# A row-wise maximum that ignores NaN: the first tile loaded as 16 and then 112 partitions

## The chip, the cores and the metric

The kernel runs on one core of a Trainium2 chip. The metric is device time in microseconds, from runs of the whole program; the median of three runs is given. The profile is of one execution, whose own time stands beside its span.

## The reference

```python
x = np.random.randn(32, 2048, 2048).astype(np.float32)
x[np.random.rand(32, 2048, 2048) < 0.1] = np.nan
np.nanmax(x, axis=-1).astype(np.float32)
```

65,536 rows of 2,048 floats (537 MB) are reduced to one float each: the largest value of the row that is not NaN. A tenth of the values is NaN.

## The kernel before

The whole input passes once through the core's on-chip memory (SBUF, 128 partitions). Each partition owns 512 rows, taken in two groups that lie one behind the other in memory (`source`, line 267). A *unit* is 256 floats, 1 KB in a partition; a row has 8 units. A *tile* is a stretch of units in all 128 partitions, at most 64 units: 64 KB in each partition, 8 MB in all. `TILES` (lines 16 to 25) lists the tiles in order. A tile is a list of loads, and a load is a tuple of steps: `(24, 40)` is one load of 64 units that is cleaned in two steps. There are 52 tiles of one load and one step at the start, the first of 16 units, the second of 48, then fifty of 64. After them the tiles have more and smaller loads, so that little work is left after the last one.

Three buffers `xt0` to `xt2` of 64 KB a partition take the tiles in turn (`number % BUFS`, line 372). For each load there are three stages:

- **Load.** SyncE (SP) issues the DMA (`load`, lines 252 to 265; the profile's line 258). A load waits until the last maximum over the tile that held the buffer before it is done (`free`, line 447), and 14 semaphores are used in turn for landings. The loads of the first `AHEAD = 3` tiles wait for nothing and are issued ahead of all else, before a barrier of the five engines (lines 273 to 286).
- **Clean.** `clean` (called in lines 396 and 397) rewrites the upper 16 bits of each float so that a NaN becomes something smaller than every number, while the order of the others is kept. ScalarE (ACT, line 295) does the first half of a step's columns, GpSimd (POOL, line 306) the second half, side by side. Both wait for the landing of the step's load.
- **Maximum.** VectorE (DVE, line 302) takes the maximum over each row's cleaned floats, one instruction for all whole rows of a step (line 431): `128x8 f32<-128x16384 f32` is eight rows in each partition. It waits for POOL's and ACT's cleaning, which count on one semaphore per step ("pair").

At the tiles that `SETTLE` (line 34) names, POOL turns finished maxima back into floats and marks rows of NaN alone; the keys are tile numbers, the values the number of tiles whose maxima are settled there. At the end a small matrix product sums the marks, two stores go out on SP, and a branch would take a slow general path if there were an infinite value or a row of NaN alone.

The order of instructions on each engine is that of the loop over tiles in line 363; the class `Order` puts in the semaphore waits, and nothing is rescheduled. The line that the change begins with is

```python
    [[(16,)], [(48,)]]
    + [[(64,)]] * 50
```

## Time and profile before

| | |
|---|---|
| runs | 1246.35 us median of 3 (1246.26 to 1246.93) |
| profiled execution | 1246.26 us, span 1244.4 us |
| VectorE, ScalarE, GpSimd busy | 1105.9, 603.7, 606.6 us |
| read from memory | 536.87 MB, 432 GB/s over the span |
| loads of 8 MB | 53 of the 102 DMAs, 31.3 us from issue to landing (median) |

A row of the timeline reads: start, length, engine, line of the kernel, operation, what it writes and reads, shapes, and in brackets the idle time of the engine just before it with what ended that time. "SPq" is the issuing of DMAs by SP. The chain of waits gives start, length and what the time went to. The landing of a load has no row of its own; it is seen where ACT's cleaning of it begins.

### The profile page before, as it was taken

How to read it: one execution, taken by the hardware profiler on the slowest of the kernel's cores; microseconds unless marked ns; L12 is line 12 of the kernel's file. 1: busy time of each engine (PE TensorE's matmuls, PEld its weight loads, DVE VectorE, ACT ScalarE, POOL GpSimd, SP SyncE). 2: the span in 40 equal slices, each digit the busy share in tenths (PEclk: the TensorE clock that was granted, in tenths of full speed). 3: DMA queues.
4: the chain of work that ended last, by engine and by line, in shares of the span. 5: the costliest groups of instructions: out<-in, count | busy, mean ns of one | idle time of the engine just before them, and what ended most of it. 6: DMA issues, size and time to landing. Idle time of an engine off the chain costs nothing.

```text
span 1244.4 us, 572 instructions
## 1 busy us (share of the span) xinstructions
PE 0.2 (0%) x2; PEld 0.1 (0%) x2; DVE 1105.9 (89%) x136; ACT 603.7 (49%) x131; POOL 606.6 (49%) x138
## 2 busy tenths in 40 slices
PE   0000000000000000000000000000000000000000
PEld 0000000000000000000000000000000000000000
DVE  1789889898898988988989889898898999999999
ACT  3354453553534535445354453544535536545556
POOL 3354453543534535445354453544535536545556
DMA  9999999999999999999999999999999999999999
GB/s 404 438 438 438 438 438 438 419 423 438 438 438 438 438 438 430 415 436 438 438 438 438 438 438 421 421 438 438 438 438 438 438 432 419 443 424 430 429 425 375
DMA packets 14688, 537.14 MB, mean 432 GB/s; under 512 B 1760, under 2 KB 1888, under 8 KB 4704
## 3 DMA queue, kind: packets, MB, share of 16 engines
q1 hardware_dynamic: 14688, 537.14, 99.9%
HBM read 536.87 MB, written 0.26 MB: 432 GB/s over the span
## 4 chain that ended last, share of the span: by engine, by line
DMA 50%; DVE 34%; POOL 14%; SPq 2%; issue 0%; ACT 0%; PE 0%
DMA xt<-in_x_dram 50%; DVE acc L302 33%; POOL xt L306 14%; SPq L258 2%; DVE parts L302 1%; POOL late L306 0%; ACT sums L295 0%; PE sums L460 0%; SPq L95 0%
## 5 line engine op out<-in xcount | busy, mean ns | idle before, releaser
L302 DVE TENSOR_REDUCE acc<-xt 128x8 f32<-128x16384 f32 (+5 forms) x95 | 1059.4, 11186 | 134.0 <-POOL xt L306 133.7
L306 POOL TENSOR_SCALAR xt<-xt 128x8192 uint16<-128x8192 int16 (+11 forms) x125 | 602.7, 4836 | 635.0 <-DMA xt<-in_x_dram 635.0
L295 ACT ACTIVATE xt<-xt 128x8192 uint16<-128x8192 int16 (+11 forms) x125 | 601.5, 4839 | 635.2 <-DMA xt<-in_x_dram 635.2
L302 DVE TENSOR_REDUCE parts<-xt 128x1 f32<-128x2048 f32 (+6 forms) x32 | 42.6, 1410 | 0.0
L302 DVE TENSOR_REDUCE xt<-xt 128x1 f32<-128x768 f32 (+1 forms) x4 | 3.7, 944 | 0.0
L302 DVE MEMSET small<- 128x1 f32 x2 | 0.1, 59 | 3.0 <-PEq L286 3.0
L295 ACT ACT_TABLE_LOAD x1 | 1.3, 1283 | 2.9 <-PEq L286 2.9
L306 POOL TENSOR_SCALAR low<-acc 128x312 f32<-128x312 f32 (+2 forms) x3 | 1.9, 626 | 0.2
L306 POOL TENSOR_SCALAR acc<-acc 128x312 uint16<-128x312 uint16 (+3 forms) x4 | 1.4, 343 | 0.3
L295 ACT ACTIVATE sums<-sums 1x22 f32<-1x22 f32 x1 | 0.1, 140 | 1.1 <-PE sums L460 1.1
L295 ACT ACTIVATE low<-low 128x491 f32<-128x491 f32 x1 | 0.6, 585 | 0.0
L460 PE MATMUL sums<-late,small 128*1 128x22 f32 x2 | 0.2, 200 | 1242.4 <-POOL late L306 1242.4
L306 POOL TENSOR_SCALAR late<-acc 128x19 f32<-128x19 f32 x1 | 0.3, 266 | 0.1
L306 POOL TENSOR_SCALAR late<-xt 128x2 f32<-128x2 f32 x1 | 0.2, 218 | 0.1
L460 PEld LDWEIGHTS sums<-late,small 128*1 128x1 f32 x2 | 0.1, 80 | 1242.4 <-issue 1242.4
L523 POOL MEMSET const-float32-0.0<- 128x1 f32 x1 | 0.1, 99 | 0.2 <-issue 0.2
L295 ACT ACTIVATE small<-small 128x1 f32<-128x1 f32 x1 | 0.2, 203 | 0.0
L302 DVE TENSOR_SCALAR acc<-acc 128x2 uint16<-128x2 uint16 x1 | 0.2, 171 | 0.0
L302 DVE TENSOR_REDUCE acc<-parts 128x19 f32<-128x57 f32 x1 | 0.2, 200 | 0.0
L295 ACT ACTIVATION_READ_ACCUMULATOR low<-low 128x1 f32 x1 | 0.2, 187 | 0.0
L295 ACT ACTIVATION_READ_ACCUMULATOR sums<-sums 1x1 f32 x1 | 0.2, 185 | 0.0
L302 DVE MEMSET parts<- 128x63 f32 x1 | 0.1, 111 | 0.0
(3 smaller groups left out, 0.3 us busy)
## 6 DMA issues: line engine op xcount, KB each, us to landing
xt<-in_x_dram SPq DMA_DIRECT2D x2, 7168.0 KB, 30.9
xt<-in_x_dram SPq DMA_DIRECT2D x2, 6144.0 KB, 24.7
xt<-in_x_dram SPq DMA_DIRECT2D x3, 4096.0 KB, 26.7
xt<-in_x_dram SPq DMA_DIRECT2D x5, 2048.0 KB, 34.4
xt<-in_x_dram SPq DMA_DIRECT2D x2, 5120.0 KB, 23.2
xt<-in_x_dram SPq DMA_DIRECT2D x3, 3072.0 KB, 33.6
xt<-in_x_dram SPq DMA_DIRECT2D x4, 1024.0 KB, 34.9
xt<-in_x_dram SPq DMA_DIRECT2D x9, 384.0 KB, 13.9
```

Of the source, the lines that this page charges most:

```text
L258: inst = nc.sync.dma_start(out=to, in_=of)
L295: lambda: nc.scalar.activation(**kw),
L302: return order.add("dve", nc.vector, lambda: do(**kw), deps)
L306: "pool", nc.gpsimd, lambda: do(**kw), deps, lane=pair, joint=pair is not None
L460: lambda: nc.tensor.matmul(sums, lhsT=ones, rhs=late, start=True, stop=True),
L523: nc = _bacc.Bacc("TRN2", target_bir_lowering=False, num_devices=1)
```

## The change

The first two tiles, of 16 and 48 units, become one tile of 64 units with one step. Its load is cut by partitions and not by columns: one DMA for partitions 0 to 15 and one for 16 to 127, each with 64 KB a partition. Both cleaning instructions of the tile wait for both DMAs. All later tiles keep their contents, and their numbers fall by one, so the buffers and the points of `SETTLE` move by a tile.

```diff
 TILES = (
-    [[(16,)], [(48,)]]
+    [[(64,)]]
     + [[(64,)]] * 50
...
 AHEAD = 3
+CORNER = 16
...
             end = at + sum(steps)
-            ahead[number, at] = load(
-                xts[number][:, at * U : end * U],
-                source(0)[:, (base + at) * U : (base + end) * U],
-                [],
-                own=True,
-            )
+            cuts = [0, P] if number else [0, CORNER, P]
+            ahead[number, at] = [
+                load(
+                    xts[number][p:q, at * U : end * U],
+                    source(0)[p:q, (base + at) * U : (base + end) * U],
+                    [],
+                    own=True,
+                )
+                for p, q in zip(cuts, cuts[1:])
+            ]
...
-                clean("A", xt[:, lo:mid], [e], pair)
-                e_clean = clean("P", xt[:, mid:hi], [e], pair)
+                clean("A", xt[:, lo:mid], e, pair)
+                e_clean = clean("P", xt[:, mid:hi], e, pair)
```

In the built program SP issues four loads ahead of the barrier (16x16384, 112x16384 and two of 128x16384 elements) where there were three. VectorE has 51 maxima of 128x8 in a row at the start, where there were one of 128x2, one of 128x6 and fifty of 128x8; ACT and POOL have one cleaning instruction fewer each.

More of the change, by code (lines that the diff above doesn't have):

```diff
@@ L385 @@
             if e is None:
-                e = load(
-                    xt[:, at * U : end * U],
-                    xg[:, (base + at) * U : (base + end) * U],
-                    before,
-                )
+                e = [
+                    load(
+                        xt[:, at * U : end * U],
+                        xg[:, (base + at) * U : (base + end) * U],
+                        before,
+                    )
+                ]
             cleaned = []
@@ L393 @@
             for i, n in enumerate(steps):
-                pair = "pair_%s_%d_%d" % (*e, i) if number >= OWN else f"pair{number % PAIRS}"
+                pair = "pair_%s_%d_%d" % (*e[0], i) if number >= OWN else f"pair{number % PAIRS}"
                 lo, mid, hi = a * U, a * U + n * U // 2, (a + n) * U
-                clean("A", xt[:, lo:mid], [e], pair)
-                e_clean = clean("P", xt[:, mid:hi], [e], pair)
+                clean("A", xt[:, lo:mid], e, pair)
+                e_clean = clean("P", xt[:, mid:hi], e, pair)
                 cleaned.append((a, a + n, e_clean))
```

## The prediction

> **What bounds the kernel now.** I read the page first (busy shares, slices, DMA line), then the waits, then the timeline of the first 62 us and of the last 250 us, and last the chain that ended last. The page:

> ```profile
> span 1244.4 us, 572 instructions
> ...
> PE 0.2 (0%) x2; PEld 0.1 (0%) x2; DVE 1105.9 (89%) x136; ACT 603.7 (49%) x131; POOL 606.6 (49%) x138
> ...
> DMA  9999999999999999999999999999999999999999
> GB/s 404 438 438 438 438 438 438 419 423 438 438 438 438 438 438 430 415 436 438 438 438 438 438 438 421 421 438 438 438 438 438 438 432 419 443 424 430 429 425 375
> ```

> The DMA engines are busy in every slice and move 438 GB/s in most. No compute engine is full: VectorE, the busiest, has 89%. Who waits for whom (total us, times, longest):

> ```profile
> ACT xt L295 <- DMA xt<-in_x_dram: 635.2, 96, 12.3
> POOL xt L306 <- DMA xt<-in_x_dram: 635.0, 97, 12.3
> DVE acc L302 <- POOL xt L306: 133.7, 53, 14.6
> ```

> ScalarE and GpSimd, which clean the data, wait for loads; VectorE waits for GpSimd, so at one remove for loads too. The timeline of the opening, the part that the change touches:

> ```profile
> 7.96 2.47 ACT L295 ACTIVATE xt<-xt 128x2048 uint16<-128x2048 int16 x1 [3.55 <-DMA xt<-in_x_dram]
> ...
> 10.50 4.42 DVE L302 TENSOR_REDUCE acc<-xt 128x2 f32<-128x4096 f32 x1 [7.32 <-POOL xt L306]
> 14.95 27.89 SPq L258 DMA_DIRECT2D xt<-in_x_dram  x2
> 22.46 6.99 ACT L295 ACTIVATE xt<-xt 128x6144 uint16<-128x6144 int16 x1 [12.03 <-DMA xt<-in_x_dram]
> ...
> 29.52 12.95 DVE L302 TENSOR_REDUCE acc<-xt 128x6 f32<-128x12288 f32 x1 [14.60 <-POOL xt L306]
> 41.79 9.25 ACT L295 ACTIVATE xt<-xt 128x8192 uint16<-128x8192 int16 x1 [12.34 <-DMA xt<-in_x_dram]
> ...
> 51.12 17.22 DVE L302 TENSOR_REDUCE acc<-xt 128x8 f32<-128x16384 f32 x1 [8.64 <-POOL xt L306]
> 61.13 9.26 ACT L295 ACTIVATE xt<-xt 128x8192 uint16<-128x8192 int16 x1 [10.09 <-DMA xt<-in_x_dram]
> ```

> A start of ACT marks a landing. The first 8 MB (16 + 48 units) is in at 22.46 us, the next 8 MB at 41.79, the next at 61.13: one full tile every 19.34 us, while VectorE needs 17.22 us for it. So VectorE catches up with the loads at 51.12 and waits some 2 us a tile from there on. Does that last to the end?

> ```profile
> 997.79 90.67 DVE L302 TENSOR_REDUCE acc<-xt 128x8 f32<-128x16384 f32 x13 [2.10 <-POOL xt L306]
> 1088.71 106.60 DVE L302 TENSOR_REDUCE acc<-xt 128x4 f32<-128x8192 f32 x29 [0.26 <-POOL xt L306]
> ```

> At 997.79 and again at 1088.71 VectorE waits for data; only then it runs through. The chain of waits closes like this:

> ```profile
> 1229.85 11.23 DMA xt<-in_x_dram
> 1241.09 0.07 issue
> 1241.16 0.48 POOL xt L306
> ```

> The last load lands at 1241.09 and 3.3 us of work follow. So **the stream of loads sets the time**. From 51 us on everything hangs on landing times; if all loads land d later, the end is d later, and if they land when they do now, nothing at the head of the kernel can change the end. The change is worth what it does to the landing of the first 8 MB, and no more.

> **The change part by part.** The sum is made against the profiled execution, 1246.26 us (span 1244.40 and 1.86 around it); the median of the runs shown is 1246.35, the same within their spread of 0.7.

> *VectorE.* Two maxima (4.42 + 12.95 = 17.37 us) become one of 17.22. It now starts after the whole tile: with unchanged landings, 22.46 + 9.25 of cleaning = 31.7, end 48.95, before the 51.12 at which tile two's maximum can start. Cost nothing, hidden under that wait; 2.2 us of cover is left, and what exceeds it would shrink later waits (2.1 us a tile) long before 997 us.

> *Cleaning.* Two steps on ACT and POOL (2.47 + 6.99) become one of 9.25, now with a second semaphore to wait for. Queued behind it is only the next tile's cleaning, 19 us later. Nothing.

> *Buffers.* Both old first tiles held a buffer each; now three full tiles are loaded ahead. The load issued at 14.95 goes up front. The one that waited for the maximum ending at 42.47 (29.52 + 12.95) now waits for 48.95. It must be queued before the third full tile has landed, at 61.13: 12 us of cover, so nothing; were it gone, each us beyond would cost one. All tile numbers fall by one and the settle steps of POOL with them; POOL is 51% idle.

> *Issues on SP.* Four loads instead of three go out before the program's barrier:

> ```profile
> L258 SPq DMA_DIRECT2D xt<-in_x_dram x9: 327/328/424, 0.7 to 126.4; - x9
> ```

> That puts 0.33 to 0.42 us before ACT's table load and the memsets, whose first customer now comes 14.5 us later than before. Nothing.

> *The two loads of the first tile.* This is what decides. How loads are spread over the engines, from the DMA view of the first 60 us:

> ```profile
> DMA packets 560, 25.17 MB, mean 419 GB/s; under 512 B 48, under 2 KB 48, under 8 KB 48
> ```

> 25.17 MB is the 2, 6, 8 and 8 MB loads: 4 x 128 = 512 packets are one per partition, and 48 = 3 x 16 small ones are one per DMA engine for each load that ended in the window. So each of 16 engines moves 8 partitions of a load, and a row of 64 KB takes one engine 19.34 / 8 = 2.42 us. New: 16 partitions, one row per engine, then 112, seven per engine. By bytes the two cost 2.42 + 16.92 = 19.34, as now.

> But all 16 engines now write into 16 neighbouring partitions at once. Every load of this trace has 128 partitions, so no row shows what that does. Bounds from the rows: if nothing is shared, 2.42 us; if all 16 rows sit behind one path with the rate of one engine, 16 x 2.42 = 38.7. In the full load, the nearest row, each path serves 128 / 16 = 8 partitions at the most even; 16 neighbours reach two such paths if these are cut in blocks of eight (eight engines on each, 19.3 us) and up to all 16 if they are dealt out singly. I take the middle in ratio, **four engines to a path**: 4 x 2.42 = 9.67 us, 7.25 more than now. The engines take their loads in order, so the 112 rows start that much later.

> [...]

> For the 112 rows, seven per engine: at best 16.92 us. Seven neighbours don't fit the groups of eight of the full load, so engines meet on some paths: with one other during four of its seven rows the slowest needs 11 rows' time, 26.6 us. I take the middle, 9 rows, 21.8 us: 4.8 more than now. A landing counts when its slowest engine is done, and that engine stays late: the stream is full and has no gap to win it back.

> **Sum**: 7.25 + 4.84 = 12.1 us; 1246.26 + 12.1 = **1258.4**. Its own range: two engines to a path and nothing lost in the second load gives +2.4 (1248.7); eight to a path and nothing lost in the second, or four with 11 rows, gives +16.9 (1263.2).

> **The rivals.**

> *Not slower: nothing is shared.* If what limits is each engine's own rate, or if a partition always falls to the same engine whatever the load, the 8 MB land at 22.46 as now, and the end is 1246.3. For it: in the full loads all 16 engines run side by side without disturbing each other, and the bytes per engine stay equal. Against: there each may simply have its own path. The point from which it decides is two engines to a path: that costs 2.42 us, just under what a measurement can tell. The start might gain: the engines could begin sooner with 16 rows to prepare than 128, at most the 0.33 to 0.42 us of an issue: 1245.9.

> *Faster by over 0.2%.* The first slice moves 404 GB/s against 438: 34 x 31.1 us is 1.06 MB, 2.4 us. That is the whole start-up loss, and 0.7 of it lies before the first issue. Even if the rest went, 1.7 us is less than 0.2%. It would take a faster stream, and 438 in most slices has not moved in 1200 us.

> *Much slower.* If the 112 partitions are dealt out like cards, so that the engines keep writing 16 neighbours at a time, all eight rows take 9.67 us: 77.4 for the tile, +58, 1304. For it: nothing here excludes it; against it: the 128-partition loads, dealt so, would not run at 438.

> **How the numbers follow.** Sharing with a limited second load (the forecast) 0.68; nothing shared 0.22; much slower 0.08; faster 0.02. A measurement of this kernel can tell about 0.2% (2.5 us) from no change, so: slower 0.76, same 0.22, faster 0.02. The range goes from the no-sharing case with its small gain, 1245.7, to the top of the forecast's own with the runs' spread on it, 1264.5; it leaves out the much slower case and the tails.

> **What would show it.** The first ACT step (128x8192) starts at 34.6 us if I am right, at 22.5 if nothing is shared, at 29.7 if only the first load suffers, at 80 in the much slower case; the second 19.3 after it, and from then on all rows of before shifted by one constant. The first load (1 MB) lands some 12 us after its issue, against 4.8 unshared (2.42 and the start-up loss). The GB/s of the first slice falls from 404 to about 240, while the DMA digits stay high. VectorE's wait ahead of the second tile's maximum stays near 2 us, and the last slices look as now. I am wrong if the steady 19.34 changes, if VectorE's idle time at 997 us is gone, or if the later loads are issued so late that a gap shows in the slices.

## The result, and the profile after

The changed kernel takes 1267.94 us (median of 6 runs, 1267.67 to 1268.38) against 1246.28 of the kernel before in the same measurement: **slower by 1.7%**, ratio 1.0173 with a 95% interval of 1.016 to 1.0186. The forecast was 1258.4 with a range to 1264.5. The sign and the place are as forecast, the size is not: +21.7 us instead of +12.1.

The page of the changed kernel, the lines that answer to those of before:

```profile
span 1265.8 us, 571 instructions
...
PE 0.2 (0%) x2; PEld 0.1 (0%) x2; DVE 1105.7 (87%) x135; ACT 603.5 (48%) x130; POOL 606.4 (48%) x137
...
DMA  9999999999999999999999999999999999999998
GB/s 215 350 454 431 435 431 431 431 433 431 433 443 443 431 435 431 431 431 433 433 433 447 437 435 431 431 431 433 431 433 441 445 431 417 442 428 436 427 426 357
```

The busy times of the engines have not moved by more than 0.2 us. All of the loss is in the first two slices of the GB/s row, 215 and 350 where 404 and 438 stood, and the digits of the DMA row don't show it: the DMA engines are busy all the time, and move about half as much (215 GB/s for 404 in the first slice). The timeline of its opening:

```profile
44.20 9.25 ACT L300 ACTIVATE xt<-xt 128x8192 uint16<-128x8192 int16 x1 [39.11 <-DMA xt<-in_x_dram]
...
53.53 17.22 DVE L307 TENSOR_REDUCE acc<-xt 128x8 f32<-128x16384 f32 x1 [49.66 <-POOL xt L311]
63.49 9.27 ACT L300 ACTIVATE xt<-xt 128x8192 uint16<-128x8192 int16 x1 [10.04 <-DMA xt<-in_x_dram]
...
72.83 17.22 DVE L307 TENSOR_REDUCE acc<-xt 128x8 f32<-128x16384 f32 x1 [2.08 <-POOL xt L311]
82.78 9.26 ACT L300 ACTIVATE xt<-xt 128x8192 uint16<-128x8192 int16 x1 [10.02 <-DMA xt<-in_x_dram]
```

The first tile is in at 44.20 us instead of 22.46, 21.74 later (34.6 was forecast); from there on a tile lands every 19.3 us, as before, and VectorE waits its 2.08 us ahead of the second. The delay stays to the end:

```profile
1019.27 90.66 DVE L307 TENSOR_REDUCE acc<-xt 128x8 f32<-128x16384 f32 x13 [2.14 <-POOL xt L311]
1110.16 106.58 DVE L307 TENSOR_REDUCE acc<-xt 128x4 f32<-128x8192 f32 x29 [0.24 <-POOL xt L311]
```

Both rows stand 21.5 us behind those of before, with the same waits. No more than 0.3 us of the delay was won back, and nothing more was lost.

How the 21.7 us are split between the two loads is seen in the issue of the first one (line 259 in the first us, from issue to landing) and in a table by stretches (start:end, length, five engines' busy time, clock, DMA share, GB/s):

```profile
DMA to landing us min/median/max: 11.8/11.8/11.8
```

```profile
0.00:12.00 12.00, 0.00 (x0) 0.00 (x0) 0.18 (x3) 1.49 (x2) 0.19 (x4) 1.00 1.16 175
12.00:44.00 32.00, 0.00 (x0) 0.00 (x0) 0.00 (x0) 0.00 (x0) 0.00 (x0) 1.00 0.91 236
44.00:63.30 19.30, 0.00 (x0) 0.00 (x0) 9.77 (x1) 9.25 (x1) 9.24 (x1) 1.00 0.99 428
```

The load of 16 partitions was issued at 0.72 and landed at 12.5; without 2.4 us for start and landing that is 9.4 us, where 9.67 had been forecast. (The 2.4 is taken from the kernel before, whose first 2 MB landed 7.2 us after their issue, with 4.84 us of moving; for a whole first tile in one load, below, it is 22.2 - 19.34 = 2.9, so the 9.4 is known to half a us.) The load of 112 partitions landed 31.7 us later, where 21.8 had been forecast. From 12 to 44 us the stream runs at 236 GB/s, about half of the 428 in the stretch after it, though these 112 partitions are almost the whole memory. (A packet's bytes and time are counted where it starts, so a share over 1 in a short stretch means nothing.)

### The profile page after: what moved, and what is told of

It reads as the page before. It is cut to its first block, busy times and chain, and to the rows that moved or that the text cites. A ratio compares the mean times of both kernels' runs of the same rounds, so it can differ in the third digit from the quotient of the medians.

```text
span 1265.8 us, 571 instructions
## 1 busy us (share of the span) xinstructions
PE 0.2 (0%) x2; PEld 0.1 (0%) x2; DVE 1105.7 (87%) x135; ACT 603.5 (48%) x130; POOL 606.4 (48%) x137
## 4 chain that ended last, share of the span: by engine, by line
DMA 49%; DVE 31%; POOL 15%; SPq 3%; another core or an unknown queue 2%; issue 0%; ACT 0%; PE 0%
DMA xt<-in_x_dram 49%; DVE acc L307 31%; POOL xt L311 15%; SPq L259 3%; ACT sums L300 0%; PE sums L467 0%; POOL late L311 0%; DVE xt L307 0%; SPq L96 0%
## 5 line engine op out<-in xcount | busy, mean ns | idle before, releaser
L307 DVE TENSOR_REDUCE acc<-xt 128x8 f32<-128x16384 f32 (+6 forms) x94 | 1059.3, 11304 | 154.9 <-POOL xt L311 154.6
L311 POOL TENSOR_SCALAR xt<-xt 128x8192 uint16<-128x8192 int16 (+12 forms) x124 | 602.5, 4873 | 656.7 <-DMA xt<-in_x_dram 656.7
L300 ACT ACTIVATE xt<-xt 128x8192 uint16<-128x8192 int16 (+12 forms) x124 | 601.3, 4876 | 656.3 <-DMA xt<-in_x_dram 656.3
L467 PE MATMUL sums<-late,small 128*1 128x22 f32 x2 | 0.2, 201 | 1263.9 <-POOL late L311 1263.9
L467 PEld LDWEIGHTS sums<-late,small 128*1 128x1 f32 x2 | 0.1, 80 | 1263.9 <-issue 1263.9
```

The source lines that it names most:

```text
L300: lambda: nc.scalar.activation(**kw),
L307: return order.add("dve", nc.vector, lambda: do(**kw), deps)
L311: "pool", nc.gpsimd, lambda: do(**kw), deps, lane=pair, joint=pair is not None
L467: lambda: nc.tensor.matmul(sums, lhsT=ones, rhs=late, start=True, stop=True),
```

## The experiments

**Theory 1** is that of the prediction: the partitions lie behind a limited number of paths, and DMA engines that write behind the same path share the rate of one. Which partitions share one is put to the test by the loads of "Each load by itself": their expectation names the grouping, their times show how far it holds, and every count of shared paths after that is worked out from it. No trace names a path; what is measured is the time of a load and of its packets, by its partitions. **Rivals**: merging the tiles costs; each load of other than 128 partitions has a price of its own; it is a matter of the cold start.

**The cut taken back, the merged tile kept.**

```diff
-            cuts = [0, P] if number else [0, CORNER, P]
+            cuts = [0, P]
```

Measured: 1246.67 us, ratio to before 1.0003 (0.9994 to 1.0012). The cleaning of the first tile starts at 22.91 us. The merged tile, its later maximum, the moved buffers and settle points cost nothing that can be told from no change. It is all in the cut.

**The cut on 2 MB instead of 8.**

```diff
-    [[(64,)]]
+    [[(16,)], [(48,)]]
     + [[(64,)]] * 50
```

> The kernel before with its two first tiles of 16 and 48 units, where only the 16 units are loaded as 16 and 112 partitions (16 KB each). Theory 1 (paths): the loss goes with the bytes that are loaded so, a quarter of 21.7: +5.4, 1251.7 us. Rival 2 (a fixed price for each load of other than 128 partitions): about +21.7 again, 1268 us. If the smaller load loses nothing: 1246.3.

Measured: 1249.81 us, ratio 1.0027 (1.0016 to 1.0039): +3.5, not the 21.7 of a fixed price, but less than a quarter of it too. The first tile:

```profile
12.07 2.47 ACT L300 ACTIVATE xt<-xt 128x2048 uint16<-128x2048 int16 x1 [7.19 <-DMA xt<-in_x_dram]
```

It lands 4.1 us later than in the kernel before (7.96). Its load of 16 partitions lands 4.7 us after its issue: with 2.4 of start-up that is 2.3 us, just a quarter of 9.4. So it is the second load that loses less than in proportion when its rows are short; the last probe comes back to that.

**The cut in the middle of the stream** (tile 20, all else in one load).

```diff
+                cuts = [0, CORNER, P] if number == 20 else [0, P]
                 e = [
                     load(
-                        xt[:, at * U : end * U],
...
+                        xt[p:q, at * U : end * U],
```

> The changed kernel with its first tile in one load, and tile 20, in the middle of the stream, loaded as 16 and then 112 partitions. Theory 1 (paths): the same loss as at the start, +19 to +22: 1265 to 1268 us, since the stream has no gap to win it back; the tile after it then lands some 41 us after the one before it instead of 19.3. Rival 3 (a matter of the cold start): 1246.3.

Measured: 1268.51 us, ratio 1.0177 (1.0161 to 1.0192), +22.2. It is no matter of the cold start, and 800 us of stream behind it win nothing back. Around the cut tile:

```profile
391.64 9.26 ACT L300 ACTIVATE xt<-xt 128x8192 uint16<-128x8192 int16 x1 [11.69 <-DMA xt<-in_x_dram]
...
431.44 9.25 ACT L300 ACTIVATE xt<-xt 128x8192 uint16<-128x8192 int16 x1 [30.53 <-DMA xt<-in_x_dram]
...
450.72 9.27 ACT L300 ACTIVATE xt<-xt 128x8192 uint16<-128x8192 int16 x1 [10.04 <-DMA xt<-in_x_dram]
```

The cut tile lands 39.8 us after the one before it, and that one is already 1.6 us late (11.69 of waiting instead of 10.05). Packets of the cut tile have begun by then: from 372 to 391.7 us the DMA share, counted where a packet starts, is 1.28, against 1.00 in the 22 us before. That they hold up the tile ahead is an estimate from these two numbers.

**Each load by itself.** The variant with one load is given additional loads ahead of everything, each waiting for the one before. A load is given by its first partition, the bound that its last one stays below, the step, and the columns.

```diff
+PROBES = (
+    (0, 16, 1, 16384),
+    (0, 61, 4, 16384),
+    (32, 93, 4, 16384),
...
+    probed = []
+    for p, q, by, cols in PROBES:
+        probed = [load(xts[0][p:q:by, 0:cols], source(0)[p:q:by, 0:cols], probed)]
```

> The variant with the first tile in one load, with twelve additional loads ahead of everything (no tile is loaded ahead of the barrier), each waiting for the one before, 64 KB a partition, so that each one's time from issue to landing can be read alone; about 2.4 us of it is start and landing. First 16 partitions, one per DMA engine: 0 to 15; every fourth from 0 to 60; every fourth from 32 to 92; every eighth from 0 to 120; every seventh from 11 to 116; every seventh from 16 to 121; every second from 0 to 30. Theory 1 with paths of four neighbours and the four neighbours 32 above: 4, 2, 1, 2, 1, 2 (on two paths alone) and 2 engines to a path, so 12.1, 7.3, 4.8, 7.3, 4.8, 7.3, 7.3 us. Paths of eight neighbours: 8, 4, 4, 2, 1 to 2, 1 to 2, 8 engines: every fourth from 0 and from 32 are the same. Rival 2 (any load of other than 128 partitions is slow in itself): all seven the same, near 12. Then larger ones: partitions 16 to 127, 0 to 111, 0 to 63, 0 to 95, 0 to 127. Theory 1: 0 to 63 reaches half of the paths, 19.3 + 2.4 = 21.8; all 128 also 21.8; 16 to 127 alone 22 to 34, as behind the 16.

The table by stretches of this kernel, one stretch per load from its issue to the next, in the order above (the length is what counts, then the DMA share and GB/s at the end):

```profile
1.48:13.06 11.58, 0.00 (x0) 0.00 (x0) 0.18 (x3) 1.45 (x2) 0.00 (x0) 1.00 0.74 91
13.06:20.55 7.49, 0.00 (x0) 0.00 (x0) 0.00 (x0) 0.00 (x0) 0.00 (x0) 1.00 0.65 140
20.55:26.09 5.54, 0.00 (x0) 0.00 (x0) 0.00 (x0) 0.00 (x0) 0.00 (x0) 1.00 0.54 189
26.09:33.53 7.44, 0.00 (x0) 0.00 (x0) 0.00 (x0) 0.00 (x0) 0.00 (x0) 1.00 0.65 141
33.53:39.12 5.59, 0.00 (x0) 0.00 (x0) 0.00 (x0) 0.00 (x0) 0.00 (x0) 1.00 0.58 188
39.12:46.21 7.09, 0.00 (x0) 0.00 (x0) 0.00 (x0) 0.00 (x0) 0.00 (x0) 1.00 0.66 148
46.21:53.89 7.68, 0.00 (x0) 0.00 (x0) 0.00 (x0) 0.00 (x0) 0.00 (x0) 1.00 0.63 137
53.89:88.17 34.28, 0.00 (x0) 0.00 (x0) 0.00 (x0) 0.00 (x0) 0.00 (x0) 1.00 0.88 214
88.17:120.95 32.78, 0.00 (x0) 0.00 (x0) 0.00 (x0) 0.00 (x0) 0.00 (x0) 1.00 0.92 224
120.95:143.81 22.86, 0.00 (x0) 0.00 (x0) 0.00 (x0) 0.00 (x0) 0.00 (x0) 1.00 0.88 183
143.81:175.71 31.90, 0.00 (x0) 0.00 (x0) 0.00 (x0) 0.00 (x0) 0.00 (x0) 1.00 0.93 197
175.71:197.68 21.97, 0.00 (x0) 0.00 (x0) 0.00 (x0) 0.00 (x0) 0.00 (x0) 1.00 0.91 382
```

The first seven loads, each of 1 MB by the same 16 engines, take 5.5, 7.1 to 7.7 or 11.6 us, and which of these is within 0.8 us of what theory 1 says from the partitions alone. Rows two and three tell it best: every fourth partition in both, from 0 two engines to a path, 7.49 us, from 32 one, 5.54. No price per load and no paths of eight neighbours make a difference between these two. Of the grouping the times show this: neighbours slow each other (0 to 15 took 11.58 us, every second from 0 to 30 7.68); partitions four apart do where 0 to 28 are loaded with 32 to 60 (7.49), and don't where 32 to 60 are loaded with 64 to 92 (5.54). The grouping of the expectation fits all seven times; that no other does is not shown. The two with one engine to a path are 0.7 us slower than expected.

The larger loads hold what was missed. Partitions 16 to 127 take 34.28 us by themselves, 31.9 beyond start and landing, as behind the 16 (31.7): no effect of the load ahead. Partitions 0 to 111 and 0 to 95 are no better, 32.8 and 31.9. Partitions 0 to 63, by theory 1 behind half of the paths, take 22.9 us for half the bytes that all 128 take 22.0 for. And the sixth row is odd: of its 16 partitions only four share paths by theory 1, but its DMA share times its length, 0.66 x 7.09 = 4.7 us, is the mean time of an engine's packet, so nearly *all* engines took twice the 2.42 us of a row (the shortest packet took 3.9).

**One more load of 1 MB in the kernel, with and without sharing.**

```diff
+    extra = load(
+        xts[2][0:16:1, :], source(0)[0:16:1, 0 : WIDE * D], [], own=True
+    )
...
-AHEAD = 3
+AHEAD = 2
...
-    free = [[] for _ in range(BUFS)]
+    free = [[], [], [extra]]
```

> The variant with the first tile in one load, with one more load ahead of it: 64 KB for each of partitions 0 to 15, into the third buffer, which is overwritten later (the third tile's load waits for it and is issued some 12 us in). Only 1 MB more to read. Theory 1 (paths, four engines on each): 4 rows of 2.42 us, 1246.7 + 9 to 10 = 1256 us. By bytes alone: 1249.1.

> The same, but the 16 partitions of the extra load are every fourth from 32 to 92, one to a path by theory 1: one row of 2.42 us and up to 0.7 of uneven start, 1249.1 to 1249.8 us. If any load of 16 partitions costs the same: as with partitions 0 to 15.

Measured: 1255.29 us with partitions 0 to 15 (ratio to before 1.0073, 1.0056 to 1.009), 1249.54 with every fourth from 32 to 92 (1.0026, 1.0016 to 1.0036). Against the 1246.67 of the variant without it, the same bytes cost 8.6 us in the one place and 2.9 in the other. The 5.7 us between them are the price of the choice of partitions in the whole kernel; only the partitions, and with them the rows that are read, are different. The 8.6 is a little under the 9 to 10 expected.

**Do two engines that share a path slow the others?**

> Twelve more loads ahead of everything, each waiting for the one before, to see whether engines that have a path to themselves are slowed by two that share one. 16 partitions, 64 KB each: every seventh from 3 (one path with two engines, 14 alone) and every third from 0 to 45 (paths with three, two and one). Theory 1a (all engines go at the pace of the fullest path): every packet of the first takes 4 to 5 us, of the second 7 us. Theory 1b (only those that share are slow): 14 packets of the first take 2.4 to 3.1 us and two 4.8. Then 32 partitions (every fourth) and 64 (every second), 64 KB: neighbours two and two or four and four to an engine gives by 1a 2 x 4.84 and 4 x 4.84 us and 2.4 for start and landing, 12.1 and 21.8; if they are dealt so that each engine keeps to one path, 7.3 and 12.1. Then partitions 16 to 127 with 16 KB and 4 KB: by 1a 14 quarters of 2.42, 8.5 + 2.4 = 10.9 us, by 1b at most 6.6 + 2.4 = 9.0. Then 16 KB for partitions 0 to 15 (4.8), for every fourth from 32 to 92 (3.0 to 3.6), for all 128 (7.2). Then 8 partitions on 8 engines: every eighth from 0 to 56 (two to a path: 7.3), every fourth from 0 to 28 (one: 4.8), and 16 partitions every fourth from 32 to 92 once more (5.5).

The same table for the first four of these loads:

```profile
1.48:8.66 7.18, 0.00 (x0) 0.00 (x0) 0.18 (x3) 1.45 (x2) 0.00 (x0) 1.00 0.47 146
8.66:19.12 10.46, 0.00 (x0) 0.00 (x0) 0.00 (x0) 0.00 (x0) 0.00 (x0) 1.00 0.73 100
19.12:27.01 7.89, 0.00 (x0) 0.00 (x0) 0.00 (x0) 0.00 (x0) 0.00 (x0) 1.00 0.70 266
27.01:39.92 12.91, 0.00 (x0) 0.00 (x0) 0.00 (x0) 0.00 (x0) 0.00 (x0) 1.00 0.80 325
```

With one shared path by theory 1 a packet took 0.47 x 7.18 = 3.4 us on average: most engines were not slowed (theory 1b). With paths of three, two and one it took 0.73 x 10.46 = 7.6 us on average, the shortest packet 6.8: those alone on a path were slowed like the rest (theory 1a). Neither theory holds for both. The 32 and 64 spread partitions took 7.9 and 12.9 us, two and four rows of 2.42 and some 3, near the 7.3 and 12.1 expected for no two engines on a path. How the partitions are dealt to the engines there is not shown.

The other loads: partitions 16 to 127 with 16 KB took 8.80 us and with 4 KB 3.53. Beyond start and landing that is 6.4 and 1.1 us, or 10.6 and 7.3 rows' time, where 64 KB took 13.2. 16 KB for partitions 0 to 15, for the spread 16 and for all 128 landed after 4.1, 2.9 and 7.3 us. Of the two loads with 8 partitions, the one with shared paths took 7.6, the other 5.2. The spread 16 once more took 5.4.

**From how many shared paths on?** A new theory, 1c: one shared path slows its own engines, a few slow all.

> Eleven additional loads ahead of everything, each waiting for the one before. 16 partitions, 64 KB each, with 1, 1, 2, 3, 4, 6, 2 and 2 paths shared by two engines (every seventh from 3; every fourth from 28, 24, 20, 16 and 8; every seventh from 16; every fifth from 17). Theory 1b (only those that share are slow): landing near 7.2 us in all, and twice as many packets near 4.7 us as shared paths, the rest near 3.1. Theory 1c (a few shared paths hold up all engines): near 3.1 for most with one, 4.7 for nearly all from two on. Then partitions 16 to 127 with 32 KB and 8 KB and all 128 with 8 KB: with 64, 16 and 4 KB the 112 took 31.9, 6.4 and 1.1 us beyond 2.4 of start and landing, so 13.2, 10.6 and 7.3 rows' time; by theory 1c the rows' time grows with their size, some 12 and 9 rows: 14.5 + 2.4 and 2.7 + 2.4 us. If it is the same for each size: 7 to 13 in both.

```profile
1.48:8.82 7.34, 0.00 (x0) 0.00 (x0) 0.18 (x3) 1.45 (x2) 0.00 (x0) 1.00 0.44 143
8.82:16.08 7.26, 0.00 (x0) 0.00 (x0) 0.00 (x0) 0.00 (x0) 0.00 (x0) 1.00 0.45 144
16.08:23.59 7.51, 0.00 (x0) 0.00 (x0) 0.00 (x0) 0.00 (x0) 0.00 (x0) 1.00 0.62 140
23.59:30.98 7.39, 0.00 (x0) 0.00 (x0) 0.00 (x0) 0.00 (x0) 0.00 (x0) 1.00 0.66 142
...
38.42:46.15 7.73, 0.00 (x0) 0.00 (x0) 0.00 (x0) 0.00 (x0) 0.00 (x0) 1.00 0.64 136
...
60.99:78.32 17.33, 0.00 (x0) 0.00 (x0) 0.00 (x0) 0.00 (x0) 0.00 (x0) 1.00 0.83 212
78.32:83.98 5.66, 0.00 (x0) 0.00 (x0) 0.00 (x0) 0.00 (x0) 0.00 (x0) 1.00 0.62 162
```

All 16-partition loads land after 7.2 to 7.7 us, as either theory has it; the share tells them apart. With one shared path (rows one and two) a packet took 0.44 x 7.34 = 3.2 us on average, with two (row three) 0.62 x 7.51 = 4.7, and with three and six 4.9. In the packets of row three the shortest took 4.2 us: all 16 engines near half rate, with two shared paths. The two other sets with two shared paths (rows left out here) agree, 4.5 and 4.7 us on average and 3.9 at the shortest. **Theory 1c holds** for these loads: from two shared paths on, the whole load runs as if each engine shared. The last two rows are partitions 16 to 127 with 32 KB and 8 KB, 14.9 and 3.3 us beyond 2.4, or 12.3 and 10.8 rows' time, where 12 and 9 were expected: rows of 64 KB lose the most (13.2), rows of 4 KB next to nothing (7.3).

The traces of the large loads show the same, row by row. Suppose that each engine takes seven neighbours of partitions 16 to 127 in order (16 to 22, 23 to 29, and so on). By the paths of theory 1, two paths are then shared while the engines are at their first, second, fifth, sixth and seventh row, and only one at the third and fourth. For partitions 0 to 111 the rows with one shared path are the fourth and fifth; with six neighbours of 0 to 95 to an engine there is none. The packets of these loads in the earlier probe, 16 at a time in the order of their starts, took on average (us; one shared path in bold):

| load | 1st | 2nd | 3rd | 4th | 5th | 6th | 7th |
|---|---|---|---|---|---|---|---|
| 16 to 127 | 4.8 | 4.7 | **3.2** | **3.8** | 4.5 | 4.6 | 4.4 |
| 0 to 111 | 4.7 | 4.7 | 4.7 | **3.3** | **3.7** | 4.6 | 4.6 |
| 0 to 95 | 4.7 | 5.1 | 4.9 | 5.1 | 4.8 | 5.1 | |

The fast rows are just those with one shared path. In the third row of 16 to 127, 14 of the 16 packets took 2.8 to 3.2 us and two 4.5 and 4.6, as theory 1c has it, and in the changed kernel itself the third row of the 112 took 3.3 us against 4.7 of the second.

**A cut by partitions that shares nothing.** Four loads of 32 partitions instead of 16 and 112.

```diff
-CORNER = 16
+FOURTH = 4
...
-            cuts = [0, P] if number else [0, CORNER, P]
+            cuts = range(1) if number else range(FOURTH)
+            by = 1 if number else FOURTH
...
-                    xts[number][p:q, at * U : end * U],
...
+                    xts[number][p:P:by, at * U : end * U],
```

> The changed kernel with its first tile still cut by partitions, but into four loads of 32, every fourth from 0, 1, 2 and 3, 64 KB each, so that each load reaches all paths. Theory 1 (paths): no sharing if the two partitions of an engine lie behind one path, as the additional load of every fourth partition showed: 1246.7 us, as with one load. Rival 2 (any cut by partitions costs) or engines that take neighbours of the load in order: each load 2 x 4.84 us, first tile in 38.7 instead of 19.3, about 1266 us.

Measured: 1247.0 us, ratio 1.0005 (0.9996 to 1.0014). The first tile lands at 23.25. Cut by partitions into four loads, but each load with every fourth partition, the tile loses nothing that can be told from no change, while two loads of neighbours lose 21.7 us. None of the variants is faster than the kernel before.

## Why the prediction was wrong in size, point by point

- *What bounds the kernel*: right. A delay of the first tile of 21.74 us is one of 21.4 in the profiled execution (1267.67 against 1246.26), and the same cut 400 us later costs as much.
- *VectorE, cleaning, buffers, issues at nothing*: right; with the cut taken back they come to 0.3 us, within the noise.
- *The 16 partitions*: right, 9.4 us where four engines to a path gave 9.67, and that the partitions decide was shown by the loads (5.5 against 7.5 us for two sets of every fourth partition) and by the price in the kernel (8.6 against 2.9 us for the same bytes). The four was the middle in ratio between the bounds from the rows, 2.4 to 38.7 us: that it came out was luck.
- *The 112 partitions*: **this step failed**. The prediction said "with one other during four of its seven rows the slowest needs 11 rows' time, 26.6 us. I take the middle, 9 rows, 21.8 us". Measured: 31.7 us, 13.1 rows. It counted for each engine alone how often it meets another. With seven neighbours to an engine and the paths of theory 1 that is in three rows at the most, fewer than the four allowed for. But two shared paths bring all 16 engines to about half rate (4.5 to 4.7 us a packet on average in three sets of 16, where 2.42 is a row's time in the full stream), and two are shared during five of the seven rows; in the other two rows an engine shares once at the most. So the slowest engine needs six rows at half rate and one at full: 6 x 4.84 + 2.42 = 31.4 us, worked out afterwards; for 0 to 95, six rows at half rate, 29.0, with 29.5 measured. The prediction put an engine's waiting for the sharing of others at nothing. And the middle between the best case and the slowest engine was taken, though the next sentence says that the slowest engine counts. Of the 9.6 us missed, 9.9 are in this term, and -0.3 in the first.
- *The range*: it ended at 1264.5 since the two upper ends, +16.9 by the one load or by the other, were never taken together; its bound of 11 rows for the second load was too low in itself. Its ends are also not quite what the text works out: 1263.2 with the spread of 0.7 is 1263.9, and the lower end was put at 1245.9.
- *The rivals*: none of them came. "Much slower" had in it that all rows of the second load suffer, but with four engines to a path in each; by theory 1 it was two engines on one or two of the paths in a row (rows of 3.2 to 4.8 us, not 9.67).

What stays open: why two shared paths hold up engines that have paths to themselves, and one doesn't; and why short rows lose less. The packets don't name partitions, so the grouping is inferred from the times of the sets, and the seven neighbours to an engine from the fast rows, which fit them. And every load here read a partition's own stretch of the input, so where it read and where it wrote never changed apart. That the limit lies in writing is therefore not shown. What speaks for it is that the sets of every fourth partition from 0 and from 32 read stretches at the same distances and still differ by 2 us.

## What to carry to other kernels

In these runs 1 MB by 16 engines took from 5.5 to 11.6 us, by its partitions alone: before cutting a load by partitions, ask which partitions the 16 engines write at the same moment. Cut by columns, as the kernel before does, or by every fourth partition with 32 to a load, which cost nothing here that can be told (1247.0 us against 1246.41); of neighbouring partitions even 112 of 128 ran at 214 GB/s, where all 128 so measured ran at 382. A busy DMA row says nothing of this; read GB/s beside it, and when a mechanism is known for one part of a change, price the other parts by its worst case too.

## What the runs showed of the hardware that was not expected

- Sets of 16 partitions with two pairs that share a path by theory 1 had no packet of 64 KB under 3.9 us, and 4.5 to 4.7 on average; in sets with one pair 11 to 14 of the 16 took 2.5 to 3.5.
- From two pairs on, more of them cost little: every seventh from 16, with two pairs by theory 1, took 7.1 us, every fourth from 0, with eight, 7.5.
- An engine seems to take seven neighbours in order of a load of 112, since just those rows are fast in which by theory 1 only one path is then shared (3.2 to 3.8 us against 4.4 to 4.8).
- 112 neighbouring partitions ran at 214 GB/s by themselves and 96 at 197, while 64 spread ones ran at 325, start and landing counted in each time.
- The load ahead of one that shares paths landed 1.6 us late too, in the middle of the stream.
